# A two-layer hybrid trunk on one Trainium2 core: the first attention head in four passes over channel quarters instead of two over halves, and the mixer's gate summed in the second and third heads instead of the first

## The chip, the cores and the metric

The kernel runs on one core of one Trainium2 chip. The metric is the device time of one execution in microseconds; the figure for the kernel before is the median of three runs.

## The reference, cut to what matters

Two layers work on 640 rows: 128 context rows (the first tile of 128, with a conditioning vector of its own) and 512 latent rows (tiles 2 to 5). Layer 0 mixes by differential attention with 8 heads, layer 1 by a gated linear recurrence; a SwiGLU block follows each. Everything that is changed lies in the attention of layer 0:

```python
def modulation(cond, w, b):                       # w_ada: 1024 x 6144
    m = jax.nn.silu(cond.reshape(-1, D_MODEL)) @ w + b
    return [t[:, None, :] for t in jnp.split(m, N_MOD, axis=-1)]

def adanorm(x, g, shift, scale):
    return rmsnorm(x, g) * (1.0 + scale) + shift
...
hp = adanorm(xp, g_norm_mix[i], mp[0], mp[1])     # shift, scale
...
qp, kp, vp = attn_project(hp, w_qkv_attn[j])      # h @ w_qkv, 8 heads
...
xp = xp + mp[2] * op                              # the mixer's gate
```

Shift and scale (the first two sixths of `w_ada`) are needed before the first projection, the gate (the third sixth, 4 MB of weights) only when the output of the whole mixer is added to the rows.

## The kernel before, in words

**Arithmetic.** Every projection works in float32 by three TensorE products: an operand is split into a rounded high part and the rest, and hi x hi, hi x lo and lo x hi are summed in PSUM. In the code `wh`/`wl` are the parts of a weight chunk (split by ScalarE and by VectorE or GpSimd in `split_raw`), `Thi`/`Tlo` those of the modulated, transposed rows hT. A chunk of `w_qkv_attn` for one head holds 2 blocks of 128 channels by 384 columns (128x768) and comes by two DMAs of 192 KB; a head has four, c0 to c3. Tile `wr` has three buffers, `wh` and `wl` six each.

**The first head.** While weights and rows arrive, the kernel works out the modulation and the first head at once, because the TensorE would have nothing else to do. `w_ada` is loaded by `half_load(m, hf, i)` in pieces of 2 blocks by 512 columns (512 KB, rows of 2 KB in DRAM), m = 0 for shift and 1 for scale, hf for the half of the 1024 output channels. `half_mm` multiplies a piece by the conditioning vectors into the PSUM tile `ada0`, `half_put` copies the sum to `adaR` (VectorE), transposes it (tile `adatp`) and forms the columns `adaC`. `unit_rows(t)` scales the rows of tile t by their inverse root mean square (squares on ScalarE, root on GpSimd, scaling on VectorE); `turned` transposes four blocks of them (`ntp`); `half_hT` turns them into four blocks of hT: multiply, add (VectorE, for some tiles GpSimd), Thi (ScalarE), Tlo (VectorE). `qkv_half(t, hf)` adds 12 products (4 blocks x 3) to the PSUM tile `psqkv` of row tile t. So there are two passes over the five row tiles, one for each half of the channels; five `psqkv` tiles stay open between them. In the second pass each tile is completed by `finish` (rotary products `t1`, `t2` with the tables on VectorE, the sum `qrows` on GpSimd, `krows` and V on ScalarE and VectorE), and its rows are turned one tile later by `turn_rows` (tile `qktp`, with QH and QL made of it).

**The gate before.** In the same second pass the table `plan` places nine loads (`gate_load`, 512 KB each but for the bias) and nine steps of eight matmuls (`gate_mm`) between the products; after the pass the sum goes by `adaR` and four small DMAs to the DRAM tile `gdram`, from which head 8 reads it.

**The other heads.** Iteration h of the head loop runs the scores, the softmax, its transposes (`ptp`) and the values (`pso`) of head h+1 and, interleaved with them, the projection of head h+2 (counted from 1). One PSUM tag `mm` of two buffers serves `psqkv`, `pso` and `psada`. `ada_parts`, which the kernel before uses in heads 7 and 8 for the shift and scale of the SwiGLU block, sums a sixth of `w_ada` in three groups of three steps:

```python
for i in range(0, len(steps), 3):
    raw = []
    for lhs, src, n in steps[i : i + 3]:
        r = wp.tile([n, D], F32, name="ar", tag="wr", bufs=3)
        nc.sync.dma_start(out=r, in_=src)
        raw.append((lhs, r))
    yield
    ps = mm_tile([P, 512], "psada")
    ...
    if i == 0:
        AC.activation(R, ps[:, :256], AF.Copy)
    else:
        VE.tensor_tensor(R, R, ps[:, :256], ALU.add)
    yield
```

Its loads take the same three `wr` buffers as the chunks of `w_qkv_attn`.

**What sets the order.** TensorE runs in program order while `strict` is on, the queue of SyncE (SP), which issues nearly all loads, too in the first head (`sp["strict"]`); on VectorE, ScalarE and GpSimd, and on SP in the later heads, a scheduler chooses the order when the kernel is built. All engines then run their instructions strictly in that order. Lines to follow: L91 is every strict load, L96 every matmul, L99 every transpose, L51 every operation of the other engines, L244 the writes to `gdram`, L286 the loads of `ada_parts`.

Of the kernel before, what the change touches and what calls it, by code (L numbers as in the profile page):

```python
# [12 lines left out]
F32 = mybir.dt.float32  # L13
# [46 lines left out]
def trunk_kernel(ctx: ExitStack, tc: tile.TileContext, I, O):  # L60
# [81 lines left out]
    def spare_slots():  # L142
        for tag, n in ((("wr", 3),) * 3 + (("wl", 6),) * 5 + (("wr", 3),) * 3 + (("wh", 6),) * 2 + (("wl", 6),) * 2 + (("wr", 3),)):
            yield tag, n
# [233 lines left out]
    half_raw = {}  # L378
    half_ps = {(0, 0): 0, (1, 0): 256, (0, 1): 0, (1, 1): 256}

    def half_load(m, hf, i):
        c0 = m * D + 512 * hf
        half_raw[m, hf, i] = load_raw(wa0[:, 2 * i : 2 * i + 2, c0 : c0 + 512], [2, 512], slots)

    def half_mm(m, hf, i):
        r = half_raw.pop((m, hf, i))
        o = half_ps[m, hf]
        for k in range(2):
            for j in range(4):
                matmul(  # L390
                    ada0[32 * j : 32 * j + 32, o : o + P],
                    cT[:, 2 * i + k, :],
                    r[:, 512 * k + P * j : 512 * k + P * j + P],
                    start=(i == 0 and k == 0),
                    stop=(i == 3 and k == 1),
                )

    def half_put(m, hf):
        o = half_ps[m, hf]
        R = cp.tile([P, 256], F32, name="adaR", tag="adaR", bufs=1)[:, :P]  # L400
        VE.tensor_copy(R, ada0[:, o : o + P])
        tp = tp_tile([P, P], "adatp")
        transpose(tp, R, ident)
        tv = tp.rearrange("p (k c) -> p k c", c=32)
        ks = slice(4 * hf, 4 * hf + 4)
        for g in range(2):
            dst = adaC[:, 0, m, g, ks]
            if m == 0:
                VE.tensor_tensor(dst, tv[:, :, g], bcol[:, m, ks], ALU.add)
            else:  # L410
                VE.scalar_tensor_tensor(dst, tv[:, :, g], 1.0, bcol[:, m, ks], ALU.add, ALU.add)
                VE.tensor_tensor(dst, dst, vcol[:, ks], ALU.mult)

    for i in range(4):
        half_load(0, 0, i)
        half_mm(0, 0, i)
# [175 lines left out]
    def attention(regA, hT, o_tiles, xs0):  # L592
        with ExitStack() as sc:
# [27 lines left out]
            def half_hT(t, hf, tp):  # L621
                g = 0 if t == 0 else 1
                ts_ = slice(t * P, (t + 1) * P)
                ks = slice(4 * hf, 4 * hf + 4)
                ha = early_tile()
                a, b = (adaC[:, 0, w, g, ks].unsqueeze(2).to_broadcast([P, 4, P]) for w in (1, 0))
                if t == 0 and hf == 0:
                    for i in range(4 * hf, 4 * hf + 4):
                        a1, b1 = (adaC[:, 0, w, 0, i : i + 1] for w in (1, 0))
                        AC.activation(hT[0][:, i, ts_], tp[:, i % 4], AF.Identity, bias=b1, scale=a1)  # L630
                VE.tensor_tensor(ha, tp, a, ALU.mult)
                (PO if t > 1 and not hf else VE).tensor_tensor(ha, ha, b, ALU.add)
                if t or hf:
                    AC.activation(hT[0][:, ks, ts_], ha, AF.Copy)
                VE.tensor_tensor(hT[1][:, ks, ts_], ha, hT[0][:, ks, ts_], ALU.subtract)

            def load_qkv(h):
                for c in range(4):
                    lo_eng = VE if (h == 0 and c in (0, 2)) or (h == 1 and c < 3) else PO
# [172 lines left out]
            def turned(t, hf):  # L812
                return turn_x(xs0[t], hf)

            xs0.append(load_x(x_in, 0))
            half_load(1, 0, 0)
            unit_rows(0)
            half_mm(1, 0, 0)
            half_put(0, 0)
            for i in range(1, 3):  # L820
                half_load(1, 0, i)
                half_mm(1, 0, i)
            xs0.append(load_x(x_in, 1))
            unit_rows(1)
            half_load(1, 0, 3)
            tp0 = turned(0, 0)
            half_mm(1, 0, 3)
            half_put(1, 0)
            loads = load_qkv(0)
            ch = [next(loads), next(loads)]  # L830
            xs0.append(load_x(x_in, 2))
            unit_rows(2)
            half_load(0, 1, 0)
            half_hT(0, 0, tp0)
            xs0.append(load_x(x_in, 3))
            unit_rows(3)
            half_load(0, 1, 1)
            xs0.append(load_x(x_in, 4))
            half_load(0, 1, 2)
            half_load(0, 1, 3)  # L840
            for i in range(3):
                half_load(1, 1, i)
            load_cache, put_cache, finish = head(0)
            pss = pss0

            def qkv_half(t, hf, between=lambda n: None):
                for n in range(12):
                    qkv_product(pss[t], ch, t, 4 * hf + n % 4, n // 4, hf == 0 and n == 0, hf == 1 and n == 11)
                    between(n)

            half_hT(1, 0, turned(1, 0))
            qkv_half(0, 0)
            half_hT(2, 0, turned(2, 0))
# [1119 lines left out]
```

## Time and profile before

| | |
|---|---|
| median of three runs | 1838.54 us (1838.1 to 1839.96) |
| the profiled execution | 1841.69 us, its span 1839.9 us |
| TensorE busy | 1778.1 us of the span, 97% |
| first product of the first head | starts at 23.00 us |
| first score matmul | starts at 75.64 us |
| TensorE's waits between these | 5.1 us |
| bytes moved by DMA | 195.27 MB |

All times of the trace count from the start of the span. A row of the timeline gives start, duration, engine, line, operation, result and operands by name, and in brackets how long the engine had been idle and who released it. A row of the table by windows gives, for each engine, busy time and the number of instructions, then the clock that TensorE was granted (1.00 is full), the share of time that the DMA engines were busy, and GB/s.

### The profile page before, as it was taken

To read this page: it belongs to the slowest core of one execution; us is meant where nothing else is said; L and a number is where in the kernel's file an instruction comes from. 1 tells how busy PE (TensorE), PEld (TensorE's weight loads), DVE (VectorE), ACT (ScalarE), POOL (GpSimd) and SP (SyncE) were. 2 spreads that over 40 slices of the span, in tenths; PEclk is the share of its full clock that TensorE was granted. 3 is DMA by queue.
4 is the path that set the end of the run, shared out by engine and by line. 5 is a ranking of instruction groups with operands and counts; after the bars stand their busy time and mean duration, and the time that the engine had idled before them with its cause. 6 is when DMAs were issued, how large, how long until landed. Compare 5 with 4: busy or idle time off the path is not lost.

```text
span 1839.9 us, 34696 instructions
## 1 busy us (share of the span) xinstructions
PE 1778.1 (97%) x13791; PEld 1634.0 (89%) x13791; DVE 1219.6 (66%) x2092; ACT 742.6 (40%) x1642; POOL 663.8 (36%) x766
## 2 busy tenths in 40 slices
PE   6999999999999999999999999999998999999997
PEld 5799999878898999899799999999777898998896
DVE  4788888756266655855776777666658656566666
ACT  3566666635131122132353333333344443433443
POOL 3344544325000000000055455555324466466562
PEclk9999999999999999999999999999999999999999
DMA  9511221554364433453532222221222323233331
GB/s 316 175 44 44 64 66 38 167 183 121 92 200 136 148 115 121 154 145 115 155 118 64 65 65 62 62 64 65 70 89 65 102 87 114 81 98 109 92 104 69
DMA packets 222856, 195.27 MB, mean 106 GB/s; under 512 B 10276, under 2 KB 176606, under 8 KB 222694
## 3 DMA queue, kind: packets, MB, share of 16 engines
q1 hardware_dynamic: 221888, 192.46, 33.7%
q8 instruction: 108, 1.77, 0.4%
q10 hardware_dynamic: 806, 0.60, 0.1%
q14 instruction: 54, 0.44, 0.1%
HBM read 185.64 MB, written 7.37 MB: 105 GB/s over the span
## 4 chain that ended last, share of the span: by engine, by line
PE 82%; DVE 8%; DMA 4%; ACT 2%; issue 2%; POOL 2%; SPq 0%; POOLq 0%; ACTq 0%; DVEq 0%
PE psgu L96 22%; PE psr L96 19%; PE psqkv L96 8%; PE psf L96 8%; PE psvg L96 5%; PE psu L96 4%; PE pso L96 2%; PE S L96 2%; PE psg L96 2%; PE pa L96 2%; PE po L96 1%; DMA wr<-w_ada 1%; DVE Q L51 1%; PE ptp L99 1%; DVE wl L51 1%
## 5 line engine op out<-in xcount | busy, mean ns | idle before, releaser
L51 ACT ACTIVATE wh<-wr 128x1024 fp32r<-128x1024 f32 (+2 forms) x224 | 217.2, 976 | 385.1 <-DMA wr<-w_ffn_in 111.3
L51 DVE TENSOR_TENSOR wl<-wr,wh 128x1024 fp32r<-128x1024 f32 (+2 forms) x148 | 183.0, 1240 | 198.4 <-ACT wh L51 197.2
L96 PE MATMUL psgu<-Thi,wh 128*128 128x320 f32 x880 | 272.5, 311 | 2.7 <-ACT wh L51 2.6
L96 PE MATMUL psgu<-Tlo,wh 128*128 128x320 f32 x880 | 272.2, 309 | 1.2 <-DVE Tlo L51 1.2
L51 POOL TENSOR_TENSOR wl<-wr,wh 128x341 fp32r<-128x341 f32 (+2 forms) x228 | 212.5, 962 | 166.0 <-ACT wh L51 165.4
L96 PE MATMUL psgu<-Thi,wl 128*128 128x320 f32 x880 | 271.4, 310 | 0.9 <-DVE wl L51 0.9
L51 POOL TENSOR_TENSOR nss<-nss 128x1 f32<-128x1 f32 x24 | 7.5, 312 | 454.0 <-ACT xr L51 438.0
L96 PEld LDWEIGHTS psgu<-Thi,wh 128*128 128x128 f32 x880 | 165.5, 188 | 5.4 <-ACT wh L51 3.5
L96 PEld LDWEIGHTS psgu<-Tlo,wh 128*128 128x128 f32 x880 | 165.6, 188 | 2.3 <-DVE Tlo L51 1.4
L96 PEld LDWEIGHTS psgu<-Thi,wl 128*128 128x128 f32 x880 | 165.3, 188 | 2.3 <-DVE wl L51 1.8
L96 PE MATMUL psr<-wh,Thi 128*128 128x512 f32 x380 | 153.3, 405 | 0.5 <-ACT Thi L51 0.5
L96 PE MATMUL psr<-wh,Tlo 128*128 128x512 f32 x380 | 149.0, 392 | 0.0
L96 PE MATMUL psr<-wl,Thi 128*128 128x512 f32 x380 | 148.9, 392 | 0.0
L96 PE MATMUL psr<-wh,gT 128*128 128x512 f32 (+1 forms) x448 | 140.4, 388 | 1.0 <-DVE gT L51 0.6
L96 PE MATMUL psf<-Thi,wh 128*128 128x320 f32 x384 | 123.1, 321 | 0.0
L51 DVE SCALAR_TENSOR_TENSOR acc<-wr,cT,acc 128x512 f32<-128x512 f32 x168 | 116.1, 744 | 6.6 <-DMA wr<-w_ada 6.6
L96 PE MATMUL psf<-Thi,wl 128*128 128x320 f32 x384 | 118.5, 308 | 0.0
L96 PE MATMUL psf<-Tlo,wh 128*128 128x320 f32 x384 | 118.4, 308 | 0.0
L96 PE MATMUL psqkv<-wh,Thi 128*128 128x384 f32 x320 | 109.8, 359 | 1.0 <-ACT Thi L51 1.0
L96 PE MATMUL psqkv<-wh,Tlo 128*128 128x384 f32 x320 | 105.9, 345 | 0.5 <-DVE Tlo L51 0.5
L96 PE MATMUL psqkv<-wl,Thi 128*128 128x384 f32 x320 | 104.5, 342 | 0.0
L51 DVE TENSOR_TENSOR rtmp<-psr,gate 128x512 f32<-128x512 f32 (+1 forms) x101 | 66.2, 678 | 55.2 <-PE psr L96 45.9
(289 smaller groups left out, 4695.7 us busy)
## 6 DMA issues: line engine op xcount, KB each, us to landing
wr<-w_ffn_in SPq DMA_DIRECT2D x176, 256.0 KB
wr<-w_ada SPq DMA_DIRECT2D x72, 512.0 KB
wr<-w_ffn_out SPq DMA_DIRECT2D x40, 512.0 KB
wr<-w_in_rec SPq DMA_DIRECT2D x64, 256.0 KB
wr<-w_qkv_attn SPq DMA_DIRECT2D x64, 192.0 KB
ar<-w_ada SPq DMA_DIRECT2D x24, 512.0 KB
gate<-gdram SPq DMA_DIRECT2D x28, 256.0 KB
wr<-w_o_attn SPq DMA_DIRECT2D x8, 512.0 KB
```

The source lines that it names most:

```text
L51: ins = op(*a, **k)
L96: in_order(nc.tensor.matmul(*a, **k))
L99: in_order(nc.tensor.transpose(*a, **k))
```

## The change

The first head works in four passes over quarters of the channels (2 blocks of 128), each with 6 products a tile. Shift and scale are loaded by quarters: 4 blocks by 256 columns a DMA, 512 KB each in rows of 1 KB. `quarter_mm` sums even and odd blocks in separate column groups, so `quarter_put` replaces the 128x128 transpose by one matmul with a constant of four columns (`strips`), which adds the two groups while it turns them. `quarter_hT` forms hT's two blocks with one VectorE operation each (multiply and add in one) straight from PSUM. The gate leaves the first head: `ada_parts([(0, 2)])` sums it in the second and third turn of the head loop, and its end (`drain`) stands at the start of that third turn. The pools of buffers that carry the early weights are used in another order (`spare_slots`). The core of the diff:

```diff
     def spare_slots():
-        for tag, n in ((("wr", 3),) * 3 + (("wl", 6),) * 5 + (("wr", 3),) * 3 + (("wh", 6),) * 2 + (("wl", 6),) * 2 + (("wr", 3),)):
-            yield tag, n
+        wr, wh, wl = ("wr", 3), ("wh", 6), ("wl", 6)
+        yield from (wr, wr, wr, wl, wl, wl, wl, wl, wh, wh, wh, wr, wr, wl, wl, wl)
...
+    def quarter_load(m, q):
+        c0 = m * D + 256 * q
+        for i in range(2):
+            quarter_raw[m, q, i] = load_raw(wa0[:, 4 * i : 4 * i + 4, c0 : c0 + 256], [4, 256], slots)
...
+    def quarter_mm(m, q):
+        o = quarter_place(m, q)
+        for i in range(2):
+            r = quarter_raw.pop((m, q, i))
+            for k in range(4):
+                for c in range(2):
+                    j = 2 * (k % 2) + c
+                    matmul(
+                        ada0[32 * j : 32 * j + 32, o : o + P],
+                        cT[:, 4 * i + k, :],
+                        r[:, 256 * k + P * c : 256 * k + P * c + P],
...
+        VE.tensor_copy(R, ada0[:, o : o + P])
+        tp = tp_tile([P, 4], "adatp")
+        matmul(tp, R, strips.rearrange("p k g -> p (k g)"), start=True, stop=True)
...
+            def quarter_hT(t, q, tp):
...
+                first = t == 0 and q == 0
+                for i in range(2):
+                    a, b = (adaC[:, 0, w, g, 2 * q + i : 2 * q + i + 1] for w in (1, 0))
+                    if first:
+                        AC.activation(hT[0][:, 2 * q + i, ts_], tp[:, i], AF.Identity, bias=b, scale=a)
+                    VE.tensor_scalar(ha[:, i], tp[:, i], a, b, ALU.mult, ALU.add)
+                if not first:
+                    AC.activation(hT[0][:, ks, ts_], ha, AF.Copy)
                 VE.tensor_tensor(hT[1][:, ks, ts_], ha, hT[0][:, ks, ts_], ALU.subtract)
...
-                    lo_eng = VE if (h == 0 and c in (0, 2)) or (h == 1 and c < 3) else PO
+                    lo_eng = VE if (h == 0 and c in (0, 3)) or (h == 1 and c < 3) else PO
...
+            for q in range(4):
+                for t in range(NT):
+                    nxt = (t + 1, q) if t + 1 < NT else (0, q + 1)
+                    quarter_hT(t, q, tp)
+                    if nxt[1] < 4:
+                        tp = turned(*nxt)
+                    for n in range(6):
+                        qkv_product(pss[t], ch, t, 2 * q + n % 2, n // 2, q == 0 and n == 0, q == 3 and n == 5)
+                    if q == 3:
+                        finish(t, pss[t])
+                        if len(late) > 1:
+                            late.pop(0)()
...
-            R = cp.tile([P, 256], F32, name="adaR", tag="adaR", bufs=1)
-            AC.activation(R, ada0[:, 0:256], AF.Copy)
-            ada_put(0, 2, R)
...
+            gate_sum = ada_parts([(0, 2)])
             for h in range(H - 1):
                 fill = project(h + 1, None if h else ch1)
+                if h == 2:
+                    drain(gate_sum)
...
+                        if h == 1:
+                            take(gate_sum, 1 if t == 1 else 2)
                         take(fill, 3)
```

Where the scheduler chooses, instructions move. ScalarE's rows between the squares of the first row tile (`early,nss<-x`, two rows a tile) and the Thi of the first tile, before:

```order
L51 ACTIVATE early,nss<-x 128x512 x2
L51 DMA stage<-lam_attn 128x256
L51 ACTIVATE early,nss<-x 128x512 x2
L51 ACT_TABLE_LOAD
L51 ACTIVATE lams<-lams 128x2
L51 ACTIVATE wh<-wr 128x768 x2
L51 ACTIVATE Thi<-ntp,adaC 128x128 x4
```

The same stretch of ScalarE after the change:

```order
L51 ACTIVATE early,nss<-x 128x512 x2
L51 DMA stage<-g_out_rec 1x128
L51 DMA stage<-b_ada 40x128
L51 DMA stage<-lam_attn 128x256
L51 ACTIVATE wh<-wr 128x768
L51 ACT_TABLE_LOAD
L51 ACTIVATE lams<-lams 128x2
L51 ACTIVATE early,nss<-x 128x512 x4
L51 ACTIVATE Thi<-ntp,adaC 128x128
L51 ACTIVATE early,nss<-x 128x512 x4
L51 ACTIVATE Thi<-ntp,adaC 128x128
```

The first chunk's split moved ahead of the `lams` step, and the squares of tiles 2 to 5 (eight rows) moved ahead of the first tile's second Thi; before, the squares of one tile stood there.

VectorE in the last pass of the first head, a stretch of somewhat over a tile, before (`t` with a number are the rotary products, QL the turned rows' low part):

```order
L51 TENSOR_TENSOR t_772<-psqkv,cosT 128x256
L51 TENSOR_TENSOR t_773<-psqkv,sinT 128x256
L51 TENSOR_TENSOR QL<-qktp,QH 128x2x128
L51 TENSOR_TENSOR wl<-wr,wh 128x768
L51 TENSOR_TENSOR Tlo<-early,Thi 128x4x128
L51 TENSOR_TENSOR t_772<-t_772,t_773 128x128
L51 TENSOR_TENSOR V<-psqkv,V 128x128
L51 TENSOR_TENSOR krows<-t_772,krows 128x2x64
```

And a stretch at the same work after the change:

```order
L51 TENSOR_TENSOR t_792<-psqkv,cosT 128x256
L51 TENSOR_TENSOR t_793<-psqkv,sinT 128x256
L51 TENSOR_TENSOR lb<-lb,lbe 128x16
L51 TENSOR_TENSOR QL<-qktp,QH 128x2x128
L51 TENSOR_SCALAR early<-ntp,adaC 128x128 x2
L51 TENSOR_TENSOR Tlo<-early,Thi 128x2x128
L51 TENSOR_TENSOR t_792<-t_792,t_793 128x128
L51 TENSOR_SCALAR omlb<-lb 128x16
L51 TENSOR_TENSOR V<-psqkv,V 128x128
L51 TENSOR_TENSOR Tlo<-early,Thi 128x2x128
L51 TENSOR_TENSOR krows<-t_792,krows 128x2x64
```

The operations of hT are half as wide and stand between the rotary product and its sum; the split of the second head's chunks (`wl`) is no longer in the last pass.

SP's queue in the second and third turn of the head loop, before, from the writes of the gate to the loads of the fourth head:

```order
L244 DMA gdram<-adaR 2x256 x4
L91 DMA wr<-w_qkv_attn 128x3x128 x6
L688 DMA new_k<-nkv 128x128
L689 DMA new_v<-nkv 128x128
L91 DMA ckr<-cache_attn_k 128x128 x2
L91 DMA wr<-w_qkv_attn 128x3x128 x8
```

After the change, from the loads of the gate's second and third group on:

```order
L91 DMA ckr<-cache_attn_k 128x128 x2
L286 DMA ar<-w_ada 128x1024 x5
L286 DMA ar<-b_ada 1x1024
L91 DMA wr<-w_qkv_attn 128x3x128 x5
L244 DMA gdram<-adaR 2x256 x4
L91 DMA wr<-w_qkv_attn 128x3x128 x9
```

All eight DMAs of the fourth head's four chunks now stand behind the last load of the gate, and the writes of the gate stand between the two DMAs of its third chunk. The first of those DMAs takes the buffer of the third group's first load.

## What the change will do to the time

> **What bounds the kernel now.** I read the page first, then the table by windows over the two places that the change touches, then TensorE's (PE's) timeline and waits in the first head, and last the groups of instructions of the other engines there. The page's first line and a row of the table by windows for the second and third heads (PE's busy time and count first, then its weight loads, VectorE (DVE), ScalarE (ACT), GpSimd (POOL), granted clock, DMA share, GB/s):
>
> ```profile
> PE 1778.1 (97%) x13791; PEld 1634.0 (89%) x13791; DVE 1219.6 (66%) x2092; ACT 742.6 (40%) x1642; POOL 663.8 (36%) x766
> 110.00:150.00 40.00, 40.00 (x271) 38.53 (x270) 33.85 (x83) 26.81 (x78) 18.89 (x36) 1.00 0.20 57
> ```
>
> PE is busy 40.00 of 40.00 us where the gate is to go, and 97% of the whole span: what is added there is paid in full, and what is idle lies mostly in the first head. PE's timeline in the first head, with the longest wait of that head in brackets:
>
> ```profile
> 23.00 1.63 PE L96 MATMUL psqkv<-wh,Thi 128*128 128x384 f32 x4
> ...
> 32.49 0.64 PE L96 MATMUL ada<-wr,cT 128*32 128x128 f32 x16
> 33.06 0.66 PE L99 MATMUL ntp<-ident,x 128*128 128x128 f32 x4
> 33.65 0.64 PE L96 MATMUL ada<-wr,cT 128*32 128x128 f32 x16
> 34.22 0.96 PE L96 MATMUL psqkv<-wh,Thi 128*128 128x384 f32 x4
> ...
> 36.51 0.64 PE L96 MATMUL ada<-wr,cT 128*32 128x128 f32 x16
> ...
> 64.29 0.64 PE L96 MATMUL ada<-ar,cT 128*32 128x256 f32 x8 [2.79 <-DMA ar<-w_ada]
> ...
> 75.64 0.22 PE L96 MATMUL S<-KP,QH 128*128 128x128 f32 x1
> ```
>
> Prices by starts: 512 KB of `w_ada` multiplied 33.06 - 32.49 = 0.57 us, four transposes 33.65 - 33.06 = 0.59, twelve products 36.51 - 34.22 = 2.29 (0.19 each). The first head runs from 23.00 to the first score matmul at 75.64; twelve products of the second head stand just before that mark in both orders, so I use it as the end. The waits for the gate's weights, and the clock around the long one:
>
> ```profile
> PE ada L96 <- DMA ar<-w_ada: 3.2, 2, 2.8
> ```
>
> ```profile
> 22.00:28.00 6.00, 5.58 (x18) 4.64 (x19) 3.65 (x9) 4.34 (x13) 4.58 (x9) 0.50 0.94 328
> 62.00:64.00 2.00, 0.00 (x0) 0.00 (x0) 2.00 (x5) 1.50 (x4) 0.69 (x2) 1.00 1.00 297
> 65.00:66.00 1.00, 1.00 (x8) 0.64 (x12) 0.85 (x3) 0.17 (x1) 0.00 (x0) 0.80 0.59 159
> 66.00:72.00 6.00, 6.00 (x26) 5.02 (x25) 2.89 (x7) 2.61 (x7) 3.05 (x5) 0.50 0.57 164
> 72.00:73.00 1.00, 1.00 (x8) 1.00 (x7) 0.00 (x0) 0.27 (x1) 0.00 (x0) 0.79 0.04 12
> ```
>
> The gate's late weights cost twice: 3.2 us of waiting, and behind it a stretch at half clock. It has 0.4 of a us in 65 to 66, six whole and 0.4 in 72 to 73 (clocks 0.80, 0.50, 0.79), about 6.8 us in which PE was busy and did half: 3.4 us lost. A stretch like it stands ahead of 28 in any case, since PE idles before the first products.
>
> **The first head, what goes.** Nine gate steps at 0.57: -5.1. The wait for their weights: -3.2, since that DMA work (4 MB) leaves the head. The second half-clock stretch: -3.4, if no idle time of that length comes back.
>
> **The first head, what comes.** From the first product on, half of the weights of shift and scale were multiplied before (8 pieces of 512 KB), now three quarters (12): 4 x 0.57 = +2.3. Six column groups are turned there instead of two, by a narrow matmul: about +0.2 each, +0.9 in all (bounds nothing and 6 x 0.33). Products and transposes are as many as before. Without waits the head would end at 75.64 - 5.1 - 3.2 - 3.4 + 2.3 + 0.9 = 67.1, 8.5 us earlier. Three waits are added; their prices come from these groups and rows (the by-shape groups of 23 to 76 for DVE, of 5 to 76 for ACT, with mean ns; POOL's of 5 to 160):
>
> ```profile
> 16.33 0.29 DVE L51 TENSOR_TENSOR stage<-stage 128x128 f32<-128x128 f32 x1 [1.67 <-DMA stage<-lam_attn]
> 18.70 0.75 DVE L51 TENSOR_SCALAR x<-x,rs 128x1024 f32<-128x1024 f32 x1 [1.76 <-POOL rs L51]
> ```
>
> ```profile
> L51 ACT ACTIVATE wh<-wr 128x768 fp32r<-128x768 f32 x10 | 8.2, 838 | 3.8 <-DMA wr<-w_qkv_attn 3.7
> L51 ACT ACTIVATE early<-x 128x512 f32<-128x512 f32 x10 | 6.2, 625 | 9.8 <-DMA x<-x_prompt 5.0 <-DMA x<-x_sample 4.5 <-POOL nss L51 0.3
> L51 ACT ACTIVATION_READ_ACCUMULATOR early<-x 128x1 f32 x10 | 1.9, 191 | 0.0
> L51 ACT ACTIVATE Thi<-ntp,adaC 128x128 fp32r<-128x128 f32 x4 | 1.5, 456 | 0.1
> ```
>
> ```profile
> L51 DVE TENSOR_TENSOR QL<-qktp,QH 128x256 fp32r<-128x256 f32 x4 | 1.7, 420 | 2.2 <-ACT QH L51 2.2
> L51 DVE TENSOR_TENSOR t<-psqkv,cosT 128x256 f32<-128x256 f32 x4 | 1.7, 416 | 0.3 <-PE psqkv L96 0.3
> L51 DVE TENSOR_TENSOR t<-psqkv,sinT 128x256 f32<-128x256 f32 x4 | 1.6, 411 | 0.0
> L51 DVE TENSOR_TENSOR t<-t,t 128x128 f32<-128x128 f32 x4 | 1.7, 420 | 0.1
> L51 DVE TENSOR_TENSOR V<-psqkv,V 128x128 fp32r<-128x128 f32 x5 | 1.4, 286 | 0.4 <-ACT V L51 0.2
> L51 DVE TENSOR_TENSOR krows<-t,krows 128x128 fp32r<-128x128 f32 x4 | 1.7, 428 | 1.8 <-ACT krows L51 1.8
> L51 DVE TENSOR_TENSOR ckd<-ckr,ckd 128x128 fp32r<-128x128 f32 x4 | 1.4, 344 | 0.0
> L51 DVE CAST ckd<-ckr 128x128 fp32r<-128x128 f32 x4 | 1.0, 245 | 1.5 <-DMA ckr<-cache_attn_k 1.5
> ```
>
> ```profile
> L51 POOL TENSOR_TENSOR qrows<-t,t 128x128 f32<-128x128 f32 x24 | 12.3, 532 | 38.6 <-DVE t L51 38.6
> L51 POOL TENSOR_TENSOR wl<-wr,wh 128x256 fp32r<-128x256 f32 x39 | 28.8, 769 | 13.6 <-ACT wh L51 13.6
> ```
>
> *Entry.* DVE works on `lam_attn` (16.33) ahead of the first chunk's `wl` and of the first scale's `adaR`, and ACT's `lams` follows it, at about 17.3 by those rows. Behind it ACT squares tiles 2 and 3 (four rows of 0.63 + 0.19 less overlap, 1.35 us a tile), one Thi, tiles 4 and 5, and only then the second Thi of the first tile: 17.3 + 2.7 + 0.46 + 2.7 + 0.46 = 23.6. DVE's Tlo stands behind the scaling of the fifth tile, which follows its squares by 1.2 (POOL) and 0.75: about 25.2. I take +1.3 us against the start at 23.00, bounds -1.5 (the squares overlap more) and +2.
>
> *Middle passes.* ACT splits five chunks among the Thi of the second and third pass, each 0.84 us (and each can wait for its weights) ahead of a Thi that PE needs. I count two as not covered, +1.7; bounds 0 and 5 x 0.84 = 4.2.
>
> *Last pass.* Between the rotary products of one tile and the next, DVE has 0.42 + 0.41 + 0.42 + 0.29 + 0.43 + 0.42 = 2.4 us, and hT's quarter: two operations from PSUM that the trace doesn't show (as V's 0.29, the nearest shape) and Tlo (as QL's 0.42), 1.0. Up to the end of the fourth tile's finish that is 3 x 2.4 + 4 x 1.0 + 2 x 0.59 for the cache = 12.4 us; PE has five tiles of 1.15 + 0.29 and four turns of 0.58, 9.5. DVE is the slower by 2.9, and behind its last sum come two `qrows` of 0.53 on POOL before PE can turn the rows. I take +4.0; bounds 0 (what DVE does ahead covers it) and 6.
>
> The head ends at 67.1 + 1.3 + 1.7 + 4.0 = 74.1, 1.5 us earlier than before.
>
> **1 KB rows.** Slices with full DMA share moved 390 to 410 GB/s in rows of 2 KB and more; the only shorter rows on the trace are those of 512 B (first window 2 to 9, second 112 to 116):
>
> ```profile
> GB/s 47 129 164 222 246 339 293 339 351 313 363 448 398 398 410 398 404 407 354 372 372 375 413 413 383 381 413 421 398 374 410 386 410 445 398 410 372 392 451 366
> ```
>
> ```profile
> GB/s 0 0 67 179 205 225 205 302 272 277 287 200 184 256 297 292 292 236 139 77 21 5 0 0 56 169 189 205 230 287 292 307 256 246 241 282 302 287 266 185
> ```
>
> Between 290 and 400, 1 KB rows may be a little slower; 8.4 MB would take 0 to 8 us longer, but the weights of later passes come ahead of need, and only the first 2 MB (0 to 2 us) precede the first product, which waits for ACT anyway. I count nothing. [...]
>
> **The second and third heads.** Three groups of `ada_parts` run in heads 7 and 8 before; the first of them and what follows:
>
> ```profile
> 344.65 1.79 PE L96 MATMUL psada<-ar,cT 128*32 128x256 f32 x24
> 346.38 0.55 PE L99 MATMUL otp<-ident,orow 128*128 128x128 f32 x3
> ```
>
> 1.73 us for three steps; nine steps are 5.2, with nothing free on PE: +5.2. So the gate's work itself only moves (-5.1, +5.2). Then a wait: the first DMA of the fourth head's chunks takes the buffer of the third group's first step, and every chunk queues behind it on SP. For a chunk on an idle queue:
>
> ```profile
> 146.41 0.55 SPq L91 DMA_DIRECT2D wr<-w_qkv_attn  x1
> ```
>
> ```profile
> 149.99 0.85 ACT L51 ACTIVATE wh<-wr 128x768 fp32r<-128x768 f32 x1 [0.30 <-DMA wr<-w_qkv_attn]
> ```
>
> Issue to landing of both halves 3.6, split 0.85 on ACT and 3 x 0.77 on POOL: 6.8 us after that step. PE has some 7.8 us left until the fourth head's first product (two steps, 18 products, 4 turns, 12 values, 4 scores, 6 transposes), so c0 is in time. c2 is not: its second half stands behind the gate's writes, which wait for DVE's sum: landed at about 9, split at 12.1, while PE wants it at 10.1; c3 must wait for c0's buffer and follows at about 14.4 where PE would be through at 13. I take +2.0, bounds 0 and 4. Queued behind: the values and the next scores. Later heads refill their lead, so nothing more.
>
> **Sum.** -1.5 + 5.2 + 2.0 = +5.7. The profiled execution took 1841.69 us, so its like would take 1847.4. It was 3.15 above the median; the forecast against the median of 1838.54 is 1844.2. A measurement of this kernel tells 0.2%, 3.7 us, from no change.
>
> **Rivals.**
>
> *The waits are covered.* DVE was busy while PE waited before too (62 to 64), which shows it can lag without deciding; if its last pass and c2 are both hidden, -1.5 - 4.0 + 5.2 = -0.3, about 1838. For it: POOL and ACT have free time. Against: in the new order DVE's hT stands between a tile's rotary products and their sum. Chance 0.22.
>
> *An early, warm start: faster.* Only 2.5 MB must land before the first tile can be modulated, against 5 MB. What delays it is `lam_attn` and the squares. If `lam_attn` lands by 14 the first product comes at about 21 and PE idles too shortly for the first half-clock stretch (22 to 28) to happen: on the covered -0.3 another -1.3 - 2 - 3 = -6.6, about 1832. It decides when the clock reads 1.00 between 23 and 28. Against: `lam_attn` is issued behind the same bytes of rows and weights. Chance 0.12.
>
> *Another half-clock stretch: slower still.* An idle time of 2.79 us sufficed at 61.5 to 64.3. If the last pass, or the fourth head's chunks, let PE idle that long once, 3.4 us are added: 1847.6, and with a late second chunk too 1850. Chance 0.12. [...]
>
> **How the numbers follow.** Forecast 0.54; rivals 0.22, 0.12, 0.12. Nearly all of the forecast and all of the last rival lie more than 3.7 us above (0.54 less 0.05, and 0.12): slower 0.61. Same: 0.22 and 0.05, 0.27. Faster: 0.12. The range goes from 1836.5, which holds the covered case, to 1850, the late case; outside it lie the fast start and the sum of all upper bounds.
>
> **What would show it.** Right: no gate loads and no half clock at 62 to 72; first product near 24; PE waits for DVE and POOL (`qktp`, Thi) in the last pass, some 4 us; first score near 74; `psada` 5.2 us between 100 and 150; a wait of PE for `wl` or `wh` of about 2 us at the fourth head's first tile. Wrong: a first score near 68 or earlier, a clock of 1.00 throughout the first products, or no wait of PE at the fourth head.

## The result, and the profile after

| | before | after |
|---|---|---|
| median | 1838.35 us (4 runs, 1838.1 to 1839.96) | 1858.68 us (4 runs, 1857.9 to 1860.0) |
| ratio after / before | | 1.0112, 95% interval 1.0099 to 1.0125 |
| profiled execution, its span | 1841.69, 1839.9 us | 1857.9, 1856.1 us |
| first score of the first head | 75.64 us | 83.88 us |
| from there to the first product of the SwiGLU block (`psgu`) | 363.76 us | 372.85 us |
| from there to the end | 1400.5 us | 1399.4 us |

The change costs 20.3 us by the medians. In the two profiles it is 16.2: +8.2 up to the first score, +9.1 in the heads behind it, -1.1 in the rest, where no line was changed. The forecast was +5.7: -1.5 and +7.2.

The page's first line after the change, with more time on PE and one per cent less of the span:

```profile
PE 1783.7 (96%) x13803; PEld 1639.4 (88%) x13803; DVE 1226.9 (66%) x2132; ACT 742.7 (40%) x1650; POOL 660.0 (36%) x763
```

PE's timeline in the first head of the changed kernel: two products of the first tile (the second with Thi, then the first with Tlo), and the first ones of the second, third and fourth pass; then the longer waits of the fourth, and the first score.

```profile
24.44 0.69 PE L96 MATMUL psqkv<-wh,Thi 128*128 128x384 f32 x1 [1.48 <-ACT Thi L51]
28.03 1.01 PE L96 MATMUL psqkv<-wh,Tlo 128*128 128x384 f32 x2 [2.26 <-DVE Tlo L51]
...
40.37 0.62 PE L96 MATMUL psqkv<-wh,Thi 128*128 128x384 f32 x2 [0.97 <-ACT Thi L51]
...
51.65 0.61 PE L96 MATMUL psqkv<-wh,Thi 128*128 128x384 f32 x2 [0.31 <-ACT Thi L51]
...
62.89 1.01 PE L96 MATMUL psqkv<-wh,Thi 128*128 128x384 f32 x2 [1.73 <-ACT Thi L51]
...
70.89 0.37 PE L99 MATMUL qktp<-ident_r,krows 128*128 128x128 f32 x2 [0.86 <-DVE krows L51]
...
72.18 0.44 PE L99 MATMUL ntp<-ident,x 128*128 128x128 f32 x2 [0.74 <-ACT K L51]
...
81.50 0.38 PE L99 MATMUL qktp<-ident_r,krows 128*128 128x128 f32 x2 [0.98 <-DVE krows L51]
...
83.88 0.22 PE L96 MATMUL S<-KP,QH 128*128 128x128 f32 x1
```

The long wait for `w_ada` is gone, and a dozen short ones for ScalarE and VectorE stand in its place. Half of the channels is through at 51.65; before, the second half began with the product at 43.43. The other half takes 32.2 us in both, although nine gate steps (5.1 us of products) are missing from it after the change. So the first head is 8.2 us behind by its middle, and its second half gains nothing from the work that was taken out.

The table by windows of the changed kernel in the same stretch (the column behind POOL is the granted clock):

```profile
24.00:31.00 7.00, 4.30 (x13) 3.70 (x14) 5.46 (x10) 1.84 (x4) 4.38 (x7) 1.00 1.11 337
...
42.00:44.00 2.00, 2.00 (x31) 1.62 (x24) 0.29 (x1) 0.00 (x0) 0.00 (x0) 0.50 1.04 314
44.00:45.00 1.00, 1.00 (x5) 1.00 (x5) 0.87 (x3) 0.10 (x1) 0.00 (x0) 0.50 1.05 354
...
63.00:69.00 6.00, 6.00 (x22) 5.81 (x23) 4.41 (x13) 2.96 (x9) 4.03 (x6) 0.50 0.31 89
...
73.00:75.00 2.00, 2.00 (x10) 1.91 (x9) 1.64 (x9) 0.20 (x1) 0.00 (x0) 0.50 0.11 33
```

Three stretches at half clock lie behind the first pass, where my sum had none: 3, 6 and 2 us in which PE was busy throughout and did half (from one pair of products to the next it is 0.64 us at 63.70, and 0.36 at 46.27), 5.5 us lost without their edges.

The second and third turn of the head loop by windows, from score to score, of the changed kernel and then of the one before:

```profile
118.21:161.49 43.28, 43.28 (x330) 38.99 (x328) 31.36 (x79) 23.42 (x71) 10.24 (x23) 1.00 0.35 112
161.49:204.03 42.54, 39.65 (x258) 36.80 (x256) 31.69 (x77) 28.92 (x79) 23.59 (x43) 1.00 0.26 75
```

```profile
110.32:148.63 38.31, 38.31 (x258) 37.03 (x256) 32.16 (x78) 25.72 (x74) 17.20 (x33) 1.00 0.18 52
148.63:186.91 38.28, 38.28 (x257) 37.02 (x256) 32.05 (x78) 25.71 (x74) 17.18 (x33) 1.00 0.18 52
```

The first row holds the gate's 72 matmuls and lasts 5.0 us longer, with PE busy throughout. The second holds no gate work, and lasts 4.3 longer: PE idles 2.9 us in it. Compared start by start with the same turn before, the whole 4.3 has arisen by 174.7 us, at the places of these waits. Who PE waits for there, by the waits of the changed kernel from 86 to 260 us (total, times, longest):

```profile
PE psqkv L96 <- POOL wl L51: 1.2, 2, 1.1
PE ptp L99 <- ACT K L51: 0.8, 1, 0.8
PE psqkv L96 <- DVE V L51: 0.6, 1, 0.6
PE psqkv L96 <- ACT wh L51: 0.3, 1, 0.3
```

### The profile page after: what moved, and what is told of

Read it like the earlier page. It is cut to its first block, busy times and chain, and to the rows that moved or that the text cites. A ratio compares the mean times of both kernels' runs of the same rounds, so it can differ in the third digit from the quotient of the medians.

```text
span 1856.1 us, 34767 instructions
## 1 busy us (share of the span) xinstructions
PE 1783.7 (96%) x13803; PEld 1639.4 (88%) x13803; DVE 1226.9 (66%) x2132; ACT 742.7 (40%) x1650; POOL 660.0 (36%) x763
## 4 chain that ended last, share of the span: by engine, by line
PE 79%; DVE 10%; DMA 4%; ACT 3%; issue 2%; POOL 2%; SPq 0%; POOLq 0%; ACTq 0%; DVEq 0%
PE psgu L96 23%; PE psr L96 16%; PE psqkv L96 8%; PE psf L96 8%; PE psvg L96 5%; PE psu L96 4%; PE S L96 2%; PE pso L96 2%; PE pa L96 2%; DVE wl L51 2%; PE psg L96 2%; PE po L96 1%; DVE Q L51 1%; ACT wh L51 1%; PE psada L96 1%
## 5 line engine op out<-in xcount | busy, mean ns | idle before, releaser
L96 PE MATMUL psqkv<-wh,Thi 128*128 128x384 f32 x320 | 114.0, 367 | 5.7 <-ACT Thi L51 4.8
```

The lines of the kernel that those rows point to most:

```text
L96: in_order(nc.tensor.matmul(*a, **k))
```

## The experiments

The theory behind them: the first head lost because PE's short waits let its clock fall, and because work at the entry stands in the wrong order; the gate's work costs its full time where it went. The rival: the first head is bound by VectorE, ScalarE and GpSimd anyway, so that what is taken off PE there brings little, whatever the passes. "Above before" is against the median of the kernel before, measured beside each group of runs. "First score" and "heads" (from there to `psgu`) come from one profile of each kernel; the kernel before has two, and its first score lies at 75.64 in one and at 72.00 in the other.

| run | median, us | above before | ratio, 95% interval | first score | heads |
|---|---|---|---|---|---|
| e1, gate moved, halves kept | 1846.15 | 8.6 | 1.0045 (1.003 to 1.006) | 71.44 | 373.37 |
| e2, after, first try at filling PE | 1873.16 | 35.6 | 1.0197 (1.0182 to 1.0211) | 98.09 | 373.32 |
| e4, before, first try at filling PE | 1850.77 | 13.2 | 1.0073 (1.006 to 1.0086) | 86.33 | 363.66 |
| e3, gate over three heads | 1859.73 | 22.1 | 1.0119 (1.0104 to 1.0135) | 85.53 | 372.64 |
| e5, PE filled, order kept | 1856.15 | 18.9 | 1.0098 (1.0082 to 1.0114) | 79.52 | 373.40 |
| e6, entry reordered | 1852.67 | 15.4 | 1.0079 (1.0064 to 1.0094) | 75.16 | 373.19 |
| e7, ScalarE reordered | 1858.46 | 21.2 | 1.0114 (1.0096 to 1.0131) | 81.27 | 374.21 |
| e8, both orders | 1852.22 | 14.9 | 1.0079 (1.0064 to 1.0094) | 75.53 | 374.63 |
| e9, quarters, gate in the first head | 1864.02 | 25.3 | 1.0135 (1.0113 to 1.0156) | 95.41 | 364.48 |
| e10, the kernel before again | 1836.5 (one run) | | | 72.00 | 364.10 |
| e11, before, gate steps later | 1840.27 | 1.6 | 1.0009 (1.0 to 1.0017) | 73.89 | 363.88 |
| e12, before, gate steps latest | 1840.77 | 2.1 | 1.0007 (0.9998 to 1.0015) | 73.66 | 363.72 |

### The gate's move alone (e1)

The kernel before with `gate_load` and `gate_mm` taken out of the first head and `ada_parts` put where the change has it:

```diff
-            for k in range(5):
-                gate_load(k)
...
+            gate_sum = ada_parts([(0, 2)])
...
+                        if h == 1:
+                            take(gate_sum, 1 if t == 1 else 2)
```

> The kernel before with one part of the change: the first head stays in two half passes, the gate goes to the second and third heads. Theory 1 (the quarter passes cost the time, by waits and half-clock stretches; the gate's move costs 5 us of TensorE and a wait at the fourth head): the first head loses the gate's 5.1 us, its 3.2 us of waiting and the half-clock stretch of 3.4, so the first score comes at 64 to 66 instead of 75.64; the later heads gain 8; together about 1835, some 4 us below the kernel before. Rival (the gate's move costs the time): 1845 or more. Rival 2 (other waits fill the first head when the gate goes): first score at 70 or later, total 1838 to 1842.

First the waits of PE in e1's first head between 22 and 72 us (its longest group, 2.6 us for `adaC`, is as before and left out), then its first score:

```profile
PE psqkv L96 <- ACT Thi L51: 2.0, 2, 1.3
PE cktp L99 <- ACT K L51: 1.6, 1, 1.6
PE psqkv L96 <- DVE Tlo L51: 1.5, 3, 1.0
PE qktp L99 <- DVE krows L51: 1.4, 2, 1.1
PE qktp L99 <- POOL qrows L51: 1.0, 1, 1.0
```

```profile
71.44 0.31 PE L96 MATMUL S<-KP,QH 128*128 128x128 f32 x1
```

The gate's 5.1 us of products and the 3.2 us of waiting for its weights are gone, and the head ends only 4.2 us earlier. New waits fill the gap: for the cache (`cktp`, 1.6), for `krows` and `qrows` (2.4 together), and 2.0 more for Thi and Tlo than the 1.5 of before, 6.0 us in all. And the half clock comes back, at another place:

```profile
68.00:72.00 4.00, 4.00 (x18) 4.00 (x16) 2.01 (x7) 1.25 (x4) 3.30 (x6) 0.57 0.50 118
```

Up to the first score that is about 2.9 us at half clock, 1.4 lost. The sum closes: -11.7 (products, wait, half clock of before) + 6.0 + 1.4 = -4.3, measured -4.2. The rival holds for this part: while the gate's products ran, the other engines caught up, and PE had nothing else to do. The heads take 9.6 us more. So with the halves kept, the move of the gate costs about 8.6 us by the median.

### The gate over three heads (e3)

```diff
-                if h == 2:
+                if h == 4:
                     drain(gate_sum)
...
-                        if h == 1:
-                            take(gate_sum, 1 if t == 1 else 2)
+                        if h in (1, 2, 3) and t in (1, 2):
+                            take(gate_sum)
```

> The changed kernel with the gate's three groups in three heads (second, third, fourth turn of the head loop, one group each, loaded in the second tile and multiplied in the third), so that the chunks of the next head are loaded in time. Theory 1: TensorE's 2.9 us of waiting at the fourth head go, the 5.2 us of matmuls stay; 2 to 3 us below the changed kernel, the first head as there (first score at 83 to 85). Rival (the wait has another cause than the buffers of the weights): a wait of 2 us or more stays at the first tile of some head.

The waits of e3 from 86 to 260 us:

```profile
PE psqkv L96 <- DVE V L51: 0.9, 1, 0.9
PE ptp L99 <- ACT K L51: 0.4, 1, 0.4
```

The wait for weights at the fourth head is gone (2.9 us of waits have become 1.3), and still the heads take 372.64 us. The three turns last 41.73, 40.86 and 40.25 us against 38.3. That is 8.0 us more than three turns before, where the changed kernel has 9.2 more; the 1.2 saved is lost again in the next turn (0.6) and behind it. The gate's products are 5.2 of it by the price of the prediction. The expected 2 to 3 us did not come: to relieve the one queue hardly pays.

### PE kept busy (e2, e4, then e5)

e2 and e4 put products of the constant `ident` between PE's steps, of the changed kernel and of the one before; nobody reads their result.

```diff
+    def keep_warm(n, o):
+        for _ in range(n):
+            matmul(ada0[:, o : o + P], ident, ident, start=True, stop=True)
```

> The changed kernel with matmuls added that compute nothing used, 104 of 128x128, at the places of the first head where TensorE waits (sized by the waits of the trace: 30 before the first scale columns, 6, 8 and 13 in the first tile, 2 to 11 at later waits); nothing is left out. Theory 1 (each stretch of half clock follows from idle time of TensorE, even from gaps of 0.3 to 1.7 us that add up, and costs 8.6 us in the first head in all): the stretches go although TensorE has more to do; first score at 76 to 79 instead of 83.88, total 5 to 8 us below the changed kernel. Rival (TensorE is held by the chains over VectorE, ScalarE and GpSimd, which don't get faster): first score within 2 us of 83.88.

> The kernel before with matmuls added that compute nothing used: 6 and 12 of 128x128 before the first products, 18 in front of the gate step whose weights come late (2.79 us of idle time); nothing is left out. Theory 1: the half-clock stretch at 65 to 72 goes (3.4 us) and most of that at 22 to 28 (up to 2.9): 3 to 6 us below the kernel before. Rival (the stretch is no consequence of the idle time, or other engines set the pace there): within 1.5 us of the kernel before.

Both failed as experiments. Such a product stands in the trace as two instructions (in e2 22 of them took 2.62 us from 76.50 on, 0.24 a product), and behind e2's longest wait it took about twice as long (12 instructions in 2.91 us from 29.43 on, 0.49 a product), so the fill was longer than many of the waits; and the scheduler gave the other engines another order (in e2 VectorE's copy `adaR` came at 28.65 instead of 19.43), so the first score came at 98.09 and 86.33. They tell nothing of the first head's clock but one thing, which comes up below.

e5 takes transposes instead (eight took 1.03 us at full clock, 0.13 each), 88 of them, and pins VectorE, ScalarE and GpSimd to the order that they have in the changed kernel:

```diff
+            transpose(ada0[:, o : o + P], ident, ident)
...
+            for eng, places in zip((nc.vector, nc.scalar, nc.gpsimd), ORDER):
+                log = traced["log"][eng]
+                for p, q in zip(places, places[1:]):
+                    tc.add_manual_dep(log[q].ins, log[p].ins.name, ...)
```

> The changed kernel with 88 transposes added that compute nothing used (0.15 us each at full clock), at the places of the first head where TensorE waits, sized to those waits; unlike the run with added matmuls, the order of the instructions on VectorE, ScalarE and GpSimd is pinned to that of the changed kernel, so that only TensorE has more to do. Nothing is left out. Theory 1 (stretches of half clock follow from idle time of TensorE, and cost some 8 us of the first head): the first head shows none or one instead of four, and the first score comes 3 to 7 us before 83.88. Rival (VectorE and ScalarE set the pace): first score within 1.5 us of 83.88, whatever the clock.

The table by windows of e5 in the last two of the stretches where the changed kernel ran at half clock, the first product of its second pass, and its first score:

```profile
60.00:64.00 4.00, 3.99 (x30) 3.58 (x28) 3.14 (x10) 1.78 (x4) 2.58 (x5) 1.00 0.51 150
64.00:68.00 4.00, 2.68 (x17) 2.08 (x18) 3.99 (x14) 1.90 (x9) 2.51 (x5) 1.00 0.58 163
...
72.00:76.00 4.00, 3.47 (x24) 2.84 (x23) 3.44 (x13) 2.49 (x7) 1.26 (x3) 1.00 0.00 0
```

```profile
40.62 0.62 PE L104 MATMUL psqkv<-wh,Thi 128*128 128x384 f32 x2 [0.43 <-ACT Thi L58]
...
79.52 0.22 PE L104 MATMUL S<-KP,QH 128*128 128x128 f32 x1
```

With the same order on the other engines and a clock of 1.00 from 28 us on, the first score comes 4.4 us earlier. So the half clock costs about 4.4 us. All of it lies behind the first pass: the second begins at 40.62, and at 40.37 without the fill, so the earlier return to full clock in the first pass brings nothing by then. That is less than the 5.5 that its stretches lost: at full speed PE waits again in part (from 64 to 68 us VectorE is busy 3.99 of 4.00, and PE 2.68).

### The orders (e6, e7, e8)

The changed kernel with pinned orders. In e6 VectorE and ScalarE do the `lam_attn` work behind the first pass, hT of the first tile comes ahead of the squares of tiles 3 to 5, and the squares have a buffer of their own. In e7 ScalarE's splits of chunks stand behind a Thi of the third and fourth pass, and eleven small vector operations behind the first head. e8 has both.

```diff
-                    row_sumsq(xt[:, 512 * i : 512 * i + 512], early_tile().rearrange("p a b -> p (a b)"))
+                if not squares:
+                    squares.append(ap_.tile([P, 2, 512], F32, name="sq", tag="QL", bufs=2))
+                sq = [row_sumsq(xt[:, 512 * i : 512 * i + 512], squares[0][:, i]) for i in range(2)]
```

> The changed kernel with another order at the start of the first head and nothing else: on VectorE and ScalarE the work on lam_attn comes after the first pass, the first tile's hT comes before the squares of tiles 3 to 5, each tile's hT right behind its scaling; the squares are written to a buffer of their own. Theory 1 (the entry, which waits for lam_attn at 17.8 and then for the squares, costs 10 us of the first half of the channels): first product at 16 to 18 instead of 22.3, no wait of 2 us for Tlo, second pass at 30 to 34 instead of 40.4, first score 5 to 9 us earlier, total 5 to 9 us below the changed kernel. Rival (the weights of the second and third pass aren't there earlier, or the last pass fills up): first score at 81 to 84.

> The changed kernel with another order in the third and last pass and nothing else: ScalarE's splits of the second head's last chunk and the third head's first chunk stand behind the Thi that they stood ahead of, and VectorE's eleven small operations for the recurrence's bounds come after the first head. Theory 1 (ScalarE stood waiting for a chunk's weights ahead of a Thi; TensorE's wait of 1.73 us behind it brought the half clock of 62 to 70): the wait and that stretch go, first score 4 to 6 us before 83.88. If only the wait goes and the clock falls all the same: 1.5 to 3 us. Rival (VectorE alone sets the last pass): within 1 us.

> The last two changes of order together. Theory 1: their gains add up, 9 to 14 us below the changed kernel, 1845 to 1850: the four passes as such don't cost the time, the order around them did, and the gate's 9 us in the later heads stay. Rival (the passes as such cost): 1852 or more.

What stands in the way at the entry: VectorE of the changed kernel.

```profile
17.78 0.29 DVE L51 TENSOR_TENSOR stage<-stage 128x128 f32<-128x128 f32 x1 [5.91 <-DMA stage<-lam_attn]
...
19.43 0.28 DVE L51 COPY adaR<-ada 128x128 f32<-128x128 f32 x1
```

And of e6, with PE's timeline behind it:

```profile
14.78 0.29 DVE L58 COPY adaR<-ada 128x128 f32<-128x128 f32 x1 [2.61 <-PE ada L104]
```

```profile
20.70 0.84 PE L104 MATMUL psqkv<-wh,Tlo 128*128 128x384 f32 x2
...
34.06 0.67 PE L104 MATMUL psqkv<-wh,Thi 128*128 128x384 f32 x2 [1.27 <-ACT Thi L58]
...
75.16 0.22 PE L104 MATMUL S<-KP,QH 128*128 128x128 f32 x1
```

VectorE of the changed kernel stands idle for 5.91 us in front of a DMA that nothing urgent needs, and the copy `adaR` of finished sums waits behind it until 19.43; in e6 it is done at 14.78. The first Tlo product comes 7.3 us earlier, the second pass 6.3, the first score 8.7, at the place of the kernel before. The median gains 5 to 6 us, and the two kernels' ranges don't overlap. That is less than 8.7: from `psgu` to the end e6's profile is 3.5 us longer than after (1402.9 and 1399.4), in a part that no edit touches. e7 took the half-clock stretch from 63 to 69 away (from 73 to 77 its clock still reads 0.57) and brought the first score to 81.27, but the next head gave 1.3 us back (`S` waits 1.2 us for K), and the median stayed. In e8 the gains don't add up: its fourth pass waits 1.40 us for `krows`, and a half-clock stretch follows (0.50 from 64 to 66). Its median of 1852.2 lies where the rival had put it: with both orders mended, the four passes and the gate's move together still cost 15 us.

### The four passes with the gate in the first head (e9)

e6's entry, with the gate's steps back in the first head, three at the end of the third pass and the others between the tiles of the fourth, and the splits of the later chunks left to the scheduler.

> The four passes alone: the order of the entry as in e6, and the gate back in the first head, its nine steps between the tiles of the fourth pass (and three ahead of it), where PE waits for the rotary products; the later heads as in the kernel before. Theory (the gate's move costs 9 us in the full heads, the four passes little): the stretch of the heads returns from 373 to about 364 us, the first score comes at 76 to 80 (75.2 in e6, plus 5.1 of gate products, less up to 4 of waits that they fill), the time falls 5 to 9 us below e6, to 1844 to 1848. Rival A (the four passes cost as much without the gate's move, for the second pass's work crowds VectorE): first score over 82 and a time as in e6, 1852 or more. Rival B (the gate's products keep the clock up and fill all waits): first score at 75 or earlier, time below 1841, no slower than the kernel before.

PE's timeline of e9 at the turn to the fourth pass (two of the nine steps wait longer than 3 us, the second 3.76):

```profile
63.08 1.08 PE L106 MATMUL ada<-ar,cT 128*32 128x256 f32 x8 [4.07 <-DMA ar<-w_ada]
```

And SP's queue there (start, time from the first to the last of the group, count):

```profile
54.28 15.71 SPq L101 DMA_DIRECT2D ar<-w_ada  x5
```

The heads came back to 364.48 us, as the theory says. The first score at 95.41 is a matter of buffers, which I had not foreseen: SP takes 15.71 us for five gate loads. By the code, rows and gate loads share the five buffers of `xo_tile` (the kernel before puts three of the nine loads into `wr`), and four passes need the rows of every tile up to the last pass, so the loads come one at a time. PE waits 13.0 us for them. So e9 doesn't price the four passes alone; e6 does better, and only with the gate elsewhere.

### The kernel before, again (e10, e11, e12)

> The kernel before, profiled once more. Its profiled execution had taken 1841.69 us, 3.2 above its median, and held a stretch at half clock from 65.4 to 72.4 us behind a wait of 2.79 us for the gate's weights. If that stretch comes in some executions only, this profile may lack it: then the first score comes at 72 to 73 and the span is near 1836, which would account for about 3.4 of the 4 us by which the medians differ more than the profiles do. If it holds it again, first score at 75 to 76, the 4 us come from elsewhere, such as the feed-forward blocks, whose length differs by 2 to 3 us between profiles of one and the same code.

e10's timeline at the wait for the gate's weights, its windows behind it, and the first score:

```profile
63.76 0.64 PE L96 MATMUL ada<-ar,cT 128*32 128x256 f32 x8 [2.16 <-DMA ar<-w_ada]
...
72.00 0.22 PE L96 MATMUL S<-KP,QH 128*128 128x128 f32 x1
```

```profile
66.00:72.00 6.00, 6.00 (x40) 5.93 (x40) 4.77 (x14) 4.73 (x14) 4.75 (x8) 1.00 0.50 144
```

The same code at the same place: a wait of 2.16 us instead of 2.79, a clock of 1.00 instead of 0.50 from 66 to 72, and a first score 3.6 us earlier. Against this profile the change costs 21.4 us (span 1834.7 to 1856.1): 11.9 up to the first score, 8.8 in the heads, 0.8 behind. That the profile of the prediction fell on the longer case is enough to account for the 4 us between the profiles and the medians.

In e11 and e12 the last two gate steps of the kernel before stand later:

```diff
-                (3, 3): "m7",
-                (3, 7): "m8",
+                (3, 11): "m7",
+                (4, 3): "m8",
```

> The kernel before, with one edit: the last two gate steps stand eight products later (behind the twelve products of the fourth row tile and behind the first four of the fifth), at about 65 and 66 us, where their weights have landed (63.76 to 64.29 in the two profiles of the kernel before). Theory: the wait of 2.2 to 2.8 us at 61.6 goes, and with it the half-clock stretch that followed it in one of the two profiles; first score at 69 to 70, time 2 to 4 us below the kernel before (1834.5 to 1836.5). Rival: the wait only moves, since VectorE is busy throughout 60 to 64 and the fifth tile's products or the turned rows come late instead; first score at 72 and no change of the time.

> As the run before, with the last two gate steps later still, behind the first four and the first eight products of the fifth row tile (about 66 and 67 us). If the weights are what PE waits for, the same gain as the run before or a few tenths more; if VectorE's lag is, no gain in either. First score at 69 to 70, time 2 to 4 us below the kernel before.

e11 at the end of its first head:

```profile
63.70 0.64 PE L96 MATMUL ada<-ar,cT 128*32 128x256 f32 x8 [0.62 <-DMA ar<-w_ada]
69.29 0.44 PE L99 MATMUL qktp<-ident,qrows 128*128 128x128 f32 x2 [1.20 <-POOL qrows L51]
70.29 0.37 PE L99 MATMUL qktp<-ident_r,krows 128*128 128x128 f32 x2 [0.56 <-DVE krows L51]
```

```profile
72.00:74.00 2.00, 2.00 (x9) 2.00 (x7) 0.70 (x2) 0.73 (x3) 2.00 (x4) 0.50 0.47 132
```

The wait of 2.2 to 2.8 us is cut to 0.62, 1.76 come back at the turned rows, and a half-clock stretch follows those. Neither run is faster than before. The weights were not all that bound that place; VectorE and GpSimd were next in line. No version here beats the kernel before.

## Why the prediction was wrong

The sign was right and the size was not: +20.3 us against a forecast of +5.7 and a range that ended 11.5 above the median before. By the marks of the profiles, up to `psgu`, 17.3 us came for 5.7, and the 11.6 us between lie in three steps. By the medians the gate's move brings 8.6 of the 20.3 (e1), and the four passes, as they were ordered, the other 11.7.

1. **The first head, what goes** (7.5 us, the step that failed). I took -5.1 for the gate's products, -3.2 for the wait and -3.4 for the clock, -11.7 in all, and wrote "Without waits the head would end at 75.64 - 5.1 - 3.2 - 3.4 + 2.3 + 0.9 = 67.1". e1 does this part alone and gains 4.2; against e10 it gains 0.6. In place of the 11.7 came 6.0 us of new waits for ScalarE, VectorE and GpSimd and 1.4 of half clock. The terms were right as busy times and wrong as gains: in the windows that I quoted PE idled while VectorE was full (62 to 64), and I read it as a sign that VectorE can lag without deciding. Behind the gate's products it was next to decide. e11 cuts just that wait to 0.62 and gains nothing. The clock's -3.4 hung on "if no idle time of that length comes back". No idle time of 2.79 us came back between the first product and the first score, and the half clock did, three times behind the first pass (once in e1); and in e10 it wasn't there to be removed.
2. **The first head, what comes** (2.2 us). I had +10.2, and from e1 to the changed kernel it is 12.4. The single terms are off by more. The entry stood at +1.3 with bounds -1.5 and +2; I had `lam_attn` landed as early as before (16.33) and it landed at 17.78 (issued 0.9 us later, and 0.6 longer on its way), with more queued behind it. e6 shows that the order there costs 8.7, 6.3 of it by the start of the second pass and the rest, with less half clock, behind it. The turn from the first pass to the second had no term; PE waits 0.41 + 0.26 + 0.97 there. The middle passes took 2.5 us of waits up to the fourth pass (0.31, 0.20, 0.25 and 1.73) for +1.7, and the last of them was the kind foreseen: on ScalarE a split, which itself waits 3.19 us for its chunk, stands ahead of Thi (e7 moved it away). The last pass was about right in size, in part by luck: seven waits, 3.7 us in all (0.86, 0.74, 0.33, 0.16, 0.18, 0.49, 0.98), for +4.0. 2.7 of them are for VectorE and GpSimd, as foreseen, and 1.1 for ScalarE, which was not.
3. **The heads** (1.9 us). The gate's products were right: 5.2 forecast, 5.0 measured. The wait at the boundary was right in kind (for `wl`, `wh`, then V) and too small: 2.0 with bounds 0 and 4, measured 4.3. Of that 2.9 are counted as waits; the other 1.4 is counted as busy time of the same 258 instructions, and lies at the same places. The chunks come late, then the values and keys behind them; e3 shows that a milder spread costs as much in all.

The 1 KB rows held up no product, as counted: after the change no wait of PE in the first head is for a DMA. Whether they move more slowly stays open: from 24 to 31 us, with full DMA share, 337 GB/s moved; before, with rows of 2 KB, it was 328 from 22 to 28 and 407 from 32 to 34, of a mix of loads.

Of the rivals, the one that came true is "another half-clock stretch", which had a chance of 0.12, and it was priced at one stretch. By e5 it is 4.4 us of the first head. It stands beside the larger cause and isn't the whole. In e4 an idle time is harmless at one place (2.70 us) and a shorter one is not at another (2.35); between the first product and the first score after the change the longest wait is 2.26, and the half clock came three times behind the first pass.

Open: how the 8.2 (or 11.9) us of the first head split exactly between entry order and clock. By the starts of the second pass, e6's order brings 6.3 ahead of it and 2.4 behind, e5's clock nothing ahead of it and 4.6 behind, so the two overlap by at most 2.4. Open too is what the four passes cost in a head whose order is right (the 15 us of e6 and e8 hold the gate's move as well; less e1's 8.6 about 6.5 is left, if the two add up), and whether four passes with the gate inside them could pay with buffers for its weights, which wasn't tried.

## What to carry to other kernels

Work taken off an engine in a stretch where it also waits is worth only what the next engine allows (in e1 4.2 of 11.7 us): ask of each removed term which engine is full there, and price the removal by that engine, or take the work out alone and look. Work moved from a stretch with waits into one that is 100% busy costs its full time and the waits that it starts (here 5.0 and 4.3 us), so the stretch that gives must gain more than the work's own length. When finer steps let work start earlier, look first at what stands ahead of it in each in-order queue: here a DMA that nobody needed held VectorE for 5.91 us.

## What the runs showed of the hardware

**Short waits can bring the half clock.** After the change it followed waits of 0.41, 0.26 and 0.97 us within 2.5 us (at 37.9 to 40.4), of 0.20, 0.25 and 1.73 (at 59.9 to 62.9), and of 0.86 and 0.74 (at 70 to 72.2); in e11 of 1.20 and 0.56. With the waits filled by transposes (e5) none of these stretches came. But waits of 1.08, 0.55 and 0.75 within 4 us (60.7 to 64.5 in e6) left the clock at 1.00:

```profile
64.00:68.00 4.00, 3.17 (x18) 2.52 (x18) 4.00 (x19) 2.28 (x8) 1.67 (x4) 1.00 0.25 72
```

In e4 a single longer wait did nothing, and a shorter one did. Its timeline, and the windows around the first and behind the second of these rows:

```profile
48.72 0.33 PE L99 MATMUL adatp<-ident,adaR 128*128 128x128 f32 x1 [2.70 <-DVE adaR L51]
...
74.47 0.64 PE L96 MATMUL ada<-ar,cT 128*32 128x256 f32 x8 [2.35 <-DMA ar<-w_ada]
```

```profile
44.00:52.00 8.00, 4.89 (x75) 4.29 (x66) 6.12 (x14) 2.24 (x6) 4.97 (x8) 1.00 0.42 121
...
75.00:81.00 6.00, 6.00 (x28) 4.65 (x25) 3.57 (x9) 3.15 (x8) 3.48 (x5) 0.50 0.32 87
```

2.70 us left the clock at 1.00 (four products took 0.94 us at 49.84, behind it), 2.35 us brought six us at 0.50 (1.65 for four at 75.03). So the length of one wait doesn't decide by itself; what does is not shown here.

**The clock column can miss a stretch.** From 24 to 31 us after the change it reads 1.00. PE's timeline there, and the same products seven us later:

```profile
24.93 0.84 PE L96 MATMUL psqkv<-wl,Thi 128*128 128x384 f32 x2
...
31.92 0.51 PE L96 MATMUL psqkv<-wl,Thi 128*128 128x384 f32 x2
```

The first pair takes 0.84 us, and so does such a pair at a clock of 0.50 (the one at 63.70 after the change). From one pair to the next it is 0.64 us at 29.90, as at 63.70, and 0.34 at 31.92. So these products ran at half speed, and the window's clock doesn't show it. The prediction had made a clock of 1.00 there a sign against itself; read by the column alone, that sign would mislead.
